# Twenty-eight experts of a PEER layer get their first product early, in plain float32

## The chip, the core and the metric

One core of a Trainium2 chip runs the whole program. The metric is the device time of one execution in microseconds (us). The engines are named as in the profile: PE (TensorE, matrix products), ACT (ScalarE), DVE (VectorE), POOL (GpSimd) and SP (SyncE, which here only issues transfers). POOL and SP both issue DMA transfers, each in a queue of its own.

## The reference, cut to what matters

Two transformer blocks on 512 tokens of width 1024. The change is in the PEER layer that ends the first block: 16384 experts, of which each token takes 8 heads x 16.

```python
def peer(h, w_query, sub_keys1, sub_keys2, expert_u, expert_v):
    q = (hf @ w_query).reshape(T, PEER_HEADS, 2, PEER_QDIM // 2)
    s1 = jnp.einsum('thc,hkc->thk', q[:, :, 0], sub_keys1)
    s2 = jnp.einsum('thc,hkc->thk', q[:, :, 1], sub_keys2)
    v1, i1 = lax.top_k(s1, PEER_TOPK)
    v2, i2 = lax.top_k(s2, PEER_TOPK)
    ...
    gate = jax.nn.softmax(vc, axis=-1)
    pre = jnp.einsum('td,tkd->tk', xb, expert_u[ib])
    a = jax.nn.gelu(pre, approximate=False) * gb
    return jnp.einsum('tk,tkd->td', a, expert_v[ib])
```

## The kernel before, in words

The 16384 experts are 128 units of 128, and the kernel calls a unit an expert `e`. For the first 384 tokens (`ND`) the layer is computed densely: for every unit a first product with `expert_u[e]` (128 experts x 384 tokens), Gelu, a multiply by a gate tile that is zero where a token did not choose the expert, and a second product with `expert_v[e]`, which is summed over all units in six PSUM banks. For the last 128 tokens the chosen rows are gathered one by one by indirect transfers, 128 of `expert_u` and 128 of `expert_v`, and DVE works each row off (`sparse`, L976).

Most products are made in three fp32r matmuls for one: both operands are split into a high part (ACT copies it, L183) and a low part (DVE subtracts, L184), and high x high, high x low and low x high are summed (`proj`, L203: 8 x 3 = 24 matmuls a unit). `wload` (L186) loads a weight unit of 512 KB on SP into one of three `wraw` buffers; `wunit` (L191) loads and splits.

The stages around the change, in program order:

- `norm_split` (L275, called at L770) computes the normalised tokens and their split `hh`, `hl`. Before it, XT is completed tile by tile (L756).
- The key search (L816 to L839): for each of 16 half heads a product with `w_query` (24 matmuls of 128x512), a piece of the modulation of the second block (`fill`, plain float32, L391), the scores against the keys (L828, plain float32) and the top 16 on DVE.
- The gates' softmax, transposes, and `pair_keys` (L878), which turns the chosen pairs into expert numbers on DVE (and POOL); `keys[0]` runs in full before the pipeline, the rest in pieces inside it.
- Gate building (L924 to L962): a pipeline of 96 items of four tokens. `g_hot` (DVE) compares, `g_wide` widens on ACT and multiplies on POOL or DVE, `g_sum` makes four plain float32 matmuls of 128x128 on PE, `g_out` copies out on ACT. Every eight items a block of 2 MB goes to DRAM (POOL's queue, L955) and a small part to the first gate tile (SP, L954).
- `u_phase` (L793) makes the first product of the first eight units (`LEAD`), with split weights.
- The loop over 128 units (L1070): in iteration e, SP loads the weights of e+10 and e+2, `prepare` (L1016) multiplies the gate into unit e+1, splits the weights of unit e+9 and the operands of unit e+1 and works off two or three gathered rows, `u_product` (L1046) makes the first product of unit e+8, `v_product` (L1054) the second of unit e (18 matmuls of 128x512).

The order of instructions on each engine is set by a list scheduler: program order is the priority, and an instruction that is ready and has its buffer may go ahead of one that is not. `tc.high_priority` lifts a part (the norm), and `pin` holds the loop's ACT and DVE instructions in program order. Each engine then runs its own list in order.

Of the kernel before, what the change touches and what calls it, by code (L numbers as in the profile page):

```python
# [107 lines left out]
def body(ctx: ExitStack, tc: tile.TileContext, a: dict, out: bass.AP, dbg=None, stop=None):  # L108
# [166 lines left out]
    def norm_split(xt, n, gcol, hh, hl, shift=None, order=None):  # L275

        with tc.high_priority():
            norm_first(xt, n, gcol, hh, hl, shift, order)

    def norm_first(xt, n, gcol, hh, hl, shift, order):  # L280
        bc = token_rstd(xt, n)
        for k in range(KT):
            h = t2(n, "nh")
            ve.scalar_tensor_tensor(h, xt[:, k], gcol[:, k:k + 1], bc, OP.mult, OP.mult)
            if shift is None:
                split_into(hh[:, k], hl[:, k], h)
            elif order is None:
                sh = shift[:, k:k + 1]
                se.activation(hh[:, k], h, AF.Identity, bias=sh)
                ve.scalar_tensor_tensor(hl[:, k], h, sh, hh[:, k].bitcast(F32), OP.add, OP.subtract)  # L290
            else:
                hs = t2(n, "nhs")
                se.activation(order[1](hs), order[0](h), AF.Identity, bias=shift[:, k:k + 1])
                split_into(hh[:, k], hl[:, k], hs)
# [469 lines left out]
    with ExitStack() as ex:  # L764
# [5 lines left out]
        norm_split(XT, T, cols[:, 8:16], hh, hl)  # L770
# [22 lines left out]
        def u_phase(e):  # L793
            ps = acc(n=ND)
            proj(ps, wunit(a["expert_u"][e]), hd_)
            t = gep.tile([128, ND], F32, name="ge")
            se.activation(t, ps, AF.Gelu)
            ge[e] = t

        with ExitStack() as gx:  # L800
# [15 lines left out]
            for hd in range(8):  # L816
                for half in range(2):
                    u = hd * 2 + half
                    keys = kp_.tile([128, 128], F32, name="keys", bufs=2)
                    gp.dma_start(keys, a["keys"][u])  # L820
                    ps = acc()
                    proj(ps, wunit(a["w_query"][u]), h)
                    fill(1 + half)
                    q = t2(name="pq")
                    se.activation(q, ps, AF.Copy)
                    st = mix([128, 4, 128], "sc")
                    for t in range(4):
                        pe.matmul(st[:, t], q[:, t * 128:(t + 1) * 128], keys, start=True, stop=True)  # L828
                    for t in range(4):
                        top16(v16[:, t, u], i16[:, t, u], st[:, t], 128, "k")  # L830
# [31 lines left out]
            hs = rows[:, RB - 1].rearrange("p (k n) -> p k n", n=128)  # L862
            ve.tensor_tensor(hs, hh[:, :, ND:].bitcast(F32), hl[:, :, ND:].bitcast(F32), OP.add)
            htok = rp.tile([128, D], F32, name="tok")
            for i in range(2):
                tps = mix([128, 4, 128], "htp")
                for k in range(4):
                    transpose(tps[:, k], hs[:, i * 4 + k])
# [3 lines left out]
        with ExitStack() as gx:  # L872
# [69 lines left out]
            def g_sum(it):  # L942
                it["ps"] = mix([128, 4, 128], "gps")
                for ti in range(4):
                    pe.matmul(it["ps"][:, ti], it["o2"][:, ti], it["o1"][:, ti], start=True, stop=True)

# [12 lines left out]
            for _ in keys[0]:  # L959
                pass  # L960
            pipeline([dict(q=th * (TG // 4) + tg, th=th, tg=tg, tok=slice(th * TG + tg * 4, th * TG + tg * 4 + 4))
                      for th in range(ND // TG) for tg in range(TG // 4)], g_hot, g_wide, g_sum, g_out)  # L962
            for e in range(LEAD):
                u_phase(e)
# [37 lines left out]
        def u_raw(e):  # L1002
            if e < NE:
# [12 lines left out]
        def prepare(eu, ev, rows_=2):  # L1016

            if ev < NE:
# [3 lines left out]
            if eu < NE:  # L1022
# [5 lines left out]
            if eu < NE:  # L1028
# [17 lines left out]
        def u_product(e):  # L1046
            if e < NE:
                ps = acc(n=ND)
                proj(ps, uw.pop(e), hd_)
                t = gep.tile([128, ND], F32, name="ge")  # L1050
                pin(se.activation(t, ps, AF.Gelu))  # L1051
                ge[e] = t
# [16 lines left out]
        prepare(NE, 0, 0)  # L1069
        for e in range(NE):  # L1070
# [4 lines left out]
            prepare(e + LEAD + 1, e + 1, 3 if e % 8 == 7 else 2)  # L1075
# [673 lines left out]
```

## Time and profile before

| what | us |
|---|---|
| median of three runs (lowest, highest) | 3473.61 (3469.06, 3474.73) |
| the profiled execution | 3477.2 |
| its span in the trace | 3475.5 |
| PE busy | 3319.4 |
| DVE busy | 2393.4 |
| ACT busy | 1265.9 |
| POOL busy | 651.4 |

The profile is of one execution, so lengths of stages and instructions are compared with its own 3477.2 us. Times in the trace count from the start of the span. A matmul's length in the trace includes its way through the array, so that matmuls in a row overlap: what one costs is read from the distance of two starts. Matmuls in fp32r appear with the type f32 in the rows.

### The profile page before, as it was taken

To read this page: it belongs to the slowest core of one execution; us is meant where nothing else is said; L and a number is where in the kernel's file an instruction comes from. 1 tells how busy PE (TensorE), PEld (TensorE's weight loads), DVE (VectorE), ACT (ScalarE), POOL (GpSimd) and SP (SyncE) were. 2 spreads that over 40 slices of the span, in tenths; PEclk is the share of its full clock that TensorE was granted. 3 is DMA by queue.
4 is the path that set the end of the run, shared out by engine and by line. 5 is a ranking of instruction groups with operands and counts; after the bars stand their busy time and mean duration, and the time that the engine had idled before them with its cause. 6 is when DMAs were issued, how large, how long until landed. Compare 5 with 4: busy or idle time off the path is not lost.

```text
span 3475.5 us, 49517 instructions
## 1 busy us (share of the span) xinstructions
PE 3319.4 (96%) x18931; PEld 2802.2 (81%) x18931; DVE 2393.4 (69%) x4746; ACT 1265.9 (36%) x2166; POOL 651.4 (19%) x676
## 2 busy tenths in 40 slices
PE   7999997679999999999999999999999999989999
PEld 4664656569999999999989887888888888878887
DVE  5544789966676776777775557587677778758776
ACT  4333213653333333333344556321211236633221
POOL 1000112653333333333311222000000002100000
PEclk9999998899999999999999999999999999999999
DMA  5345572468878888788842222121221211023331
GB/s 193 109 138 185 157 234 83 162 234 289 286 278 290 278 283 290 271 286 285 282 165 80 71 71 77 50 92 61 67 61 58 70 32 38 14 70 113 97 97 55
DMA packets 145676, 526.05 MB, mean 151 GB/s; under 512 B 17628, under 2 KB 20540, under 8 KB 143904
## 3 DMA queue, kind: packets, MB, share of 16 engines
q1 hardware_dynamic: 92880, 318.69, 28.1%
q0 software_dynamic: 52560, 204.21, 16.3%
q8 instruction: 149, 2.44, 0.3%
q14 instruction: 87, 0.71, 0.1%
HBM read 491.21 MB, written 34.10 MB: 151 GB/s over the span
## 4 chain that ended last, share of the span: by engine, by line
PE 86%; DVE 6%; DMA 3%; issue 2%; ACT 2%; POOL 1%; SPq 0%; DVEq 0%; POOLq 0%; ACTq 0%
PE pv L1061 15%; PE acc L206 12%; PE acc L208 12%; PE acc L207 12%; PE acc L232 9%; PE pd L199 3%; PE pd L201 3%; PE pd L200 3%; PE pt L347 2%; PE mod L391 2%; DMA mraw<-in_w_mod_dram 2%; DVE eb L927 1%; PE on L1351 1%; PE mix L232 1%; PE s L1312 1%
## 5 line engine op out<-in xcount | busy, mean ns | idle before, releaser
L206 PE MATMUL acc<-hh,wh 128*128 128x384 f32 (+1 forms) x1952 | 718.2, 369 | 5.2 <-DVE cg L1156 2.2
L208 PE MATMUL acc<-hh,wl 128*128 128x384 f32 (+1 forms) x1952 | 716.3, 367 | 6.0 <-DVE wl L184 6.0
L207 PE MATMUL acc<-hl,wh 128*128 128x384 f32 (+1 forms) x1952 | 715.3, 366 | 0.0
L206 PEld LDWEIGHTS acc<-hh,wh 128*128 128x128 f32 x1952 | 368.2, 189 | 64.3 <-issue 16.3
L208 PEld LDWEIGHTS acc<-hh,wl 128*128 128x128 f32 x1952 | 368.1, 189 | 53.5 <-issue 6.4
L207 PEld LDWEIGHTS acc<-hl,wh 128*128 128x128 f32 x1952 | 368.8, 189 | 46.3 <-issue 3.9
L183 ACT ACTIVATE wh<-wraw 128x1024 fp32r<-128x1024 f32 (+1 forms) x197 | 207.5, 1055 | 447.0 <-PE acc L207 249.8
L1061 PE MATMUL pv<-vh,ah 128*128 128x512 f32 x768 | 302.7, 394 | 9.5 <-DMA vraw<-in_expert_v_dram 9.5
L184 DVE TENSOR_TENSOR wl<-wraw,wh 128x1024 fp32r<-128x1024 f32 (+1 forms) x197 | 242.7, 1233 | 97.8 <-ACT wh L183 94.1
L1061 PE MATMUL pv<-vh,al 128*128 128x512 f32 x768 | 301.7, 393 | 0.0
L1061 PE MATMUL pv<-vl,ah 128*128 128x512 f32 x768 | 299.7, 390 | 0.0
L980 POOL DMA_INDIRECT rows<-in_expert_v_dram,sidx x128 | 174.3, 1362 | 312.2 <-DVE tok L995 276.8
L980 POOL DMA_INDIRECT rows<-in_expert_u_rows_dram,sidx x128 | 174.5, 1363 | 302.8 <-DVE rows L985 279.5
L1029 DVE TENSOR_TENSOR wl<-wraw,wh 128x1024 fp32r<-128x1024 f32 x120 | 149.8, 1249 | 96.5 <-ACT wh L1025 96.5
L1037 DVE TENSOR_TENSOR al<-ge,ah 128x384 fp32r<-128x384 f32 x128 | 71.4, 558 | 203.4 <-ACT ah L1035 203.4
L232 PE MATMUL acc<-wh,hh 128*128 128x256 f32 (+1 forms) x624 | 194.9, 313 | 3.9 <-ACT hh L183 2.3
L232 PE MATMUL acc<-wh,hl 128*128 128x256 f32 (+1 forms) x624 | 193.1, 309 | 0.0
L232 PE MATMUL acc<-wl,hh 128*128 128x256 f32 (+1 forms) x624 | 192.4, 308 | 0.0
L1051 ACT ACTIVATE ge<-acc 128x384 f32<-128x384 f32 x120 | 58.9, 491 | 356.6 <-PE acc L208 356.6
L1035 ACT ACTIVATE ah<-ge 128x384 fp32r<-128x384 f32 x128 | 67.0, 523 | 308.8 <-PE pv L1061 298.9
L1061 PEld LDWEIGHTS pv<-vh,ah 128*128 128x128 f32 x768 | 144.7, 189 | 35.3 <-ACT vh L1036 9.8
L1061 PEld LDWEIGHTS pv<-vh,al 128*128 128x128 f32 x768 | 144.7, 188 | 33.3
(452 smaller groups left out, 7282.3 us busy)
## 6 DMA issues: line engine op xcount, KB each, us to landing
wraw<-in_expert_u_dram SPq DMA_DIRECT2D x128, 512.0 KB, 5.4
vraw<-in_expert_v_dram SPq DMA_DIRECT2D x128, 512.0 KB, 4.0
mraw<-in_w_mod_dram SPq DMA_DIRECT2D x96, 512.0 KB, 4.3
wraw<-in_ffn_up_dram SPq DMA_DIRECT2D x88, 512.0 KB, 3.6
gt<-gdr POOLq DMA_DIRECT2D x31, 768.0 KB, 8.0
wraw<-in_ffn_down_dram SPq DMA_DIRECT2D x44, 512.0 KB, 3.7
gdr<-rows POOLq DMA_DIRECT2D x6, 2048.0 KB, 6.7
gdr<-gst POOLq DMA_DIRECT2D x6, 2048.0 KB, 7.6
```

The source lines that it names most:

```text
L183: se.activation(hi, src, AF.Copy)
L184: ve.tensor_tensor(lo, src, hi.bitcast(F32), OP.subtract)
L199: pe.matmul(ps, wh[i], xh[i], start=i == 0, stop=False)
L200: pe.matmul(ps, wh[i], xl[i], start=False, stop=False)
L201: pe.matmul(ps, wl[i], xh[i], start=False, stop=i == n - 1)
L206: pe.matmul(ps, wh[:, k], hh[:, k], start=k == 0, stop=False)
L207: pe.matmul(ps, wh[:, k], hl[:, k], start=False, stop=False)
L208: pe.matmul(ps, wl[:, k], hh[:, k], start=False, stop=k == KT - 1)
L232: pe.matmul(ps[:, i], x[:, k, s], y, start=k == 0 and i == 0 and x is hh and y is wh, stop=k == KT - 1 and i == nt - 1 and y is wl)
L980: gp.indirect_dma_start(r, None, src, bass.IndirectOffsetOnAxis(ap=sidx[:, k:k + 1], axis=0))
L1029: pin(ve.tensor_tensor(wl, raw, wh.bitcast(F32), OP.subtract))
L1061: pe.matmul(sums[t][hf], x[:, s], y[:, d], start=e == 0 and y is vh and x is ah, stop=e == NE - 1 and x is al)
```

## The change

28 units get their first product early. `early_products` is a generator of steps: for each unit it loads the raw weights and makes eight plain float32 matmuls of 128x384 with the unsplit tokens `hf`, one a step, with Gelu in the last step. `ahead(n)` takes n steps: 4 after each of the 16 query products, 10 at each of the four stops of `keys[0]`, 1 or 2 after each `g_sum`, and what is left after the pipeline. The first eight units are the LEAD units, whose `u_phase` goes; the other 20 (`SP`, units 9, 14, 20, 25, ... 113, in steps of five and six) are written to DRAM by POOL and read back by SP where the loop made their product before. For these 20 the loop neither loads nor splits `expert_u`.

The unsplit tokens are kept by writing them over XT, so XT is first stored in DRAM (`xdr1`, SP) and read back in iterations 96 to 103. The transposes for the last 128 tokens read `hf`, and the addition that rebuilt them from `hh` and `hl` goes. The gathered rows are dealt out anew: one in an iteration whose `prepare` has no weight to split, 2.38 on average in the others.

```diff
--- before.py
+++ after.py
@@ -272,15 +272,15 @@
                       start=True, stop=True)
         return bc
 
-    def norm_split(xt, n, gcol, hh, hl, shift=None, order=None):
+    def norm_split(xt, n, gcol, hh, hl, shift=None, order=None, keep=False):
 
         with tc.high_priority():
-            norm_first(xt, n, gcol, hh, hl, shift, order)
-
-    def norm_first(xt, n, gcol, hh, hl, shift, order):
+            norm_first(xt, n, gcol, hh, hl, shift, order, keep)
+
+    def norm_first(xt, n, gcol, hh, hl, shift, order, keep):
         bc = token_rstd(xt, n)
         for k in range(KT):
-            h = t2(n, "nh")
+            h = xt[:, k] if keep else t2(n, "nh")
             ve.scalar_tensor_tensor(h, xt[:, k], gcol[:, k:k + 1], bc, OP.mult, OP.mult)
             if shift is None:
                 split_into(hh[:, k], hl[:, k], h)
@@ -767,7 +767,12 @@
         pmod = pool(pp, "pmod", 1, space=PS)
         ph["mix"] = pool(pp, "pmixp", 4, space=PS)
         hh, hl = split_tile("h"), split_tile("l")
-        norm_split(XT, T, cols[:, 8:16], hh, hl)
+
+        xdr1 = dp.tile([KT, 128, T], F32, name="xdr1")
+        for k in range(KT):
+            sy.dma_start(xdr1[k], XT[:, k])
+        norm_split(XT, T, cols[:, 8:16], hh, hl, keep=True)
+        hf = XT
 
         ND, TS = T - 128, T // 128 - 1
         LEAD, RB = 8, 5
@@ -790,12 +795,33 @@
         hd_ = (hh[:, :, :ND], hl[:, :, :ND])
         ge = {}
 
-        def u_phase(e):
-            ps = acc(n=ND)
-            proj(ps, wunit(a["expert_u"][e]), hd_)
-            t = gep.tile([128, ND], F32, name="ge")
-            se.activation(t, ps, AF.Gelu)
-            ge[e] = t
+
+
+        SP = [LEAD + 1 + i * 11 // 2 for i in range(20)]
+        gedr = dp.tile([len(SP), 128, ND], F32, name="gedr")
+
+        def early_products(es):
+
+            for e in es:
+                raw = wload(a["expert_u"][e], [128, KT, 128])
+                ps = acc(n=ND)
+                for k in range(KT):
+                    pe.matmul(ps, raw[:, k], hf[:, k, :ND], start=k == 0, stop=k == KT - 1)
+                    if k < KT - 1:
+                        yield
+                t = gep.tile([128, ND], F32, name="ge") if e < LEAD else t2(ND, "gs")
+                se.activation(t, ps, AF.Gelu)
+                if e < LEAD:
+                    ge[e] = t
+                else:
+                    gp.dma_start(gedr[SP.index(e)], t)
+                yield
+
+        early = early_products(list(range(LEAD)) + SP)
+
+        def ahead(n):
+            for _ in range(n):
+                next(early, None)
 
         with ExitStack() as gx:
             mp_ = pool(gx, "mod")
@@ -821,6 +847,7 @@
                     ps = acc()
                     proj(ps, wunit(a["w_query"][u]), h)
                     fill(1 + half)
+                    ahead(4)
                     q = t2(name="pq")
                     se.activation(q, ps, AF.Copy)
                     st = mix([128, 4, 128], "sc")
@@ -859,13 +886,11 @@
                     ve.tensor_copy(gT[:, t * 128:(t + 1) * 128], tps)
                 ve.tensor_copy(ib16[:, t], i16[:, t])
 
-            hs = rows[:, RB - 1].rearrange("p (k n) -> p k n", n=128)
-            ve.tensor_tensor(hs, hh[:, :, ND:].bitcast(F32), hl[:, :, ND:].bitcast(F32), OP.add)
             htok = rp.tile([128, D], F32, name="tok")
             for i in range(2):
                 tps = mix([128, 4, 128], "htp")
                 for k in range(4):
-                    transpose(tps[:, k], hs[:, i * 4 + k])
+                    transpose(tps[:, k], hf[:, i * 4 + k, ND:])
                 se.activation(htok[:, i * 512:i * 512 + 512], tps.rearrange("p k n -> p (k n)"), AF.Copy)
             fill(25)
 
@@ -943,6 +968,7 @@
                 it["ps"] = mix([128, 4, 128], "gps")
                 for ti in range(4):
                     pe.matmul(it["ps"][:, ti], it["o2"][:, ti], it["o1"][:, ti], start=True, stop=True)
+                ahead(1 + (it["q"] % 4 == 3))
 
             def g_out(it):
                 th, tg = it["th"], it["tg"]
@@ -957,11 +983,10 @@
             gsts = {}
             keys = [pair_keys(t, gp if t else ve) for t in range(4)]
             for _ in keys[0]:
-                pass
+                ahead(10)
             pipeline([dict(q=th * (TG // 4) + tg, th=th, tg=tg, tok=slice(th * TG + tg * 4, th * TG + tg * 4 + 4))
                       for th in range(ND // TG) for tg in range(TG // 4)], g_hot, g_wide, g_sum, g_out)
-            for e in range(LEAD):
-                u_phase(e)
+            ahead(8 * len(SP))
 
         pp.close()
         b1.close()
@@ -1000,7 +1025,7 @@
         step = sparse()
 
         def u_raw(e):
-            if e < NE:
+            if e < NE and e not in SP:
                 uw[e] = wload(a["expert_u"][e], [128, KT, 128])
 
         def v_raw(e):
@@ -1015,17 +1040,18 @@
 
         def prepare(eu, ev, rows_=2):
 
+            wh = None
             if ev < NE:
                 x = ge.pop(ev)
                 pin(ve.tensor_tensor(x.rearrange("p (g t) -> p g t", t=TG), x.rearrange("p (g t) -> p g t", t=TG),
                                      gts[ev // NGR % 2][:, :, ev % NGR], OP.mult))
-            if eu < NE:
+            if eu in uw:
                 raw = uw.pop(eu)
                 wh, wl = [wp.tile([128, KT, 128], F32R, name=n, bufs=WB) for n in ("wh", "wl")]
                 pin(se.activation(wh, raw, AF.Copy))
             if rows_:
                 next(step, None)
-            if eu < NE:
+            if wh is not None:
                 pin(ve.tensor_tensor(wl, raw, wh.bitcast(F32), OP.subtract))
                 uw[eu] = wh, wl
             if ev < NE:
@@ -1045,11 +1071,13 @@
 
         def u_product(e):
             if e < NE:
-                ps = acc(n=ND)
-                proj(ps, uw.pop(e), hd_)
-                t = gep.tile([128, ND], F32, name="ge")
-                pin(se.activation(t, ps, AF.Gelu))
-                ge[e] = t
+                ge[e] = t = gep.tile([128, ND], F32, name="ge")
+                if e in SP:
+                    sy.dma_start(t, gedr[SP.index(e)])
+                else:
+                    ps = acc(n=ND)
+                    proj(ps, uw.pop(e), hd_)
+                    pin(se.activation(t, ps, AF.Gelu))
 
         def v_product(e):
             ah, al, vh, vl = vw.pop(e)
@@ -1067,12 +1095,19 @@
         v_raw(1)
         prepare(LEAD, NE, 0)
         prepare(NE, 0, 0)
+        XT = x_tiles("XT")
+        due = 0
         for e in range(NE):
             if e % NGR == 0:
                 gates(e // NGR + 1)
             u_raw(e + LEAD + 2)
             v_raw(e + 2)
-            prepare(e + LEAD + 1, e + 1, 3 if e % 8 == 7 else 2)
+            if 96 <= e < 96 + KT:
+                sy.dma_start(XT[:, e - 96], xdr1[e - 96])
+
+            due += 100 if e + LEAD + 1 in SP else 238
+            prepare(e + LEAD + 1, e + 1, due // 100)
+            due %= 100
             u_product(e + LEAD)
             v_product(e)
         for _ in step:
```

## Rows read from the trace of the kernel before

**Rows 1.** The page: busy us, share of the span and instructions by engine

```profile
PE 3319.4 (96%) x18931; PEld 2802.2 (81%) x18931; DVE 2393.4 (69%) x4746; ACT 1265.9 (36%) x2166; POOL 651.4 (19%) x676
```

**Rows 2.** Stretches: length, busy PE, PEld, DVE, ACT, POOL, then clock, DMA share, GB/s

```profile
379.00:528.00 149.00, 147.24 (x692) 91.31 (x691) 128.56 (x736) 29.73 (x39) 24.51 (x70) 1.00 0.62 204
528.00:567.20 39.20, 34.40 (x196) 31.03 (x194) 36.57 (x131) 13.50 (x18) 6.43 (x10) 1.00 0.31 97
567.20:675.00 107.80, 66.78 (x417) 61.90 (x417) 100.07 (x117) 56.40 (x100) 61.40 (x41) 0.78 0.27 111
675.00:748.60 73.60, 51.63 (x380) 46.34 (x378) 53.48 (x62) 52.35 (x94) 45.99 (x42) 0.95 0.51 201
748.60:762.60 14.00, 4.51 (x25) 4.18 (x25) 1.15 (x3) 1.64 (x3) 1.67 (x2) 0.84 0.81 309
762.60:1797.30 1034.70, 1034.66 (x5162) 938.57 (x5163) 729.14 (x899) 367.43 (x509) 376.30 (x281) 1.00 0.80 279
```

**Rows 3.** The chain of waits: start us, length, what; two iterations of the loop

```profile
782.41 4.12 PE pv L1061 x18
790.77 4.12 PE pv L1061 x18
```

**Rows 4.** Chain of waits in gate building, 568 to 748 us, shares by line

```profile
by line: DVE eb L927 21.2%; issue 19.3%; POOL o L939 14.8%; PE gps L945 9.2%; DVE o L939 8.9%; ACT o L937 4.8%; DMA gdr<-rows 4.0%; DVE eq L904 2.9%; DVE wl L1029 2.2%; DVE ic L888 2.1%; ACT rows L952 1.4%; POOL rows L980 1.3%; ACT gst L952
```

**Rows 5.** PE's groups of the whole run: the sums of gate building

```profile
L945 PE MATMUL gps<-o,o 128*128 128x128 f32 x768 | 112.4, 305 | 56.9 <-POOL o L939 29.6 <-DVE o L939 19.1 <-ACT o L937 7.3
```

**Rows 6.** PE in order of time, 91 to 98 us

```profile
91.41 1.02 PE L567 MATMUL mix<-cT,wqk_m 128*128 128x512 f32 x2
...
98.27 1.05 PE L578 MATMUL kp<-wqk_m,cT 128*128 128x128 f32 x8
```

**Rows 7.** PE in order of time, 601 to 603 us

```profile
601.39 1.95 PE L945 MATMUL gps<-o,o 128*128 128x128 f32 x16
603.10 0.42 PE L208 MATMUL acc<-hh,wl 128*128 128x384 f32 x1
```

**Rows 8.** DVE's groups in ten loop iterations, 1000 to 1083.7 us

```profile
L985 DVE SCALAR_TENSOR_TENSOR rows<-rows,tok 128x1024 f32<-128x1024 f32 x22 | 26.8, 1221 | 0.0
...
L1043 DVE TENSOR_TENSOR vl<-vraw,vh 128x1024 fp32r<-128x1024 f32 x10 | 12.2, 1221 | 0.0
...
L1037 DVE TENSOR_TENSOR al<-ge,ah 128x384 fp32r<-128x384 f32 x10 | 5.6, 558 | 16.8 <-ACT ah L1035 16.8
```

**Rows 9.** DMA issues of the whole run: KB each, us to landing

```profile
xdr<-XT SPq DMA_DIRECT2D x8, 256.0 KB, 2.3
```

**Rows 10.** DVE in order of time, 368 to 377 us

```profile
368.64 0.69 DVE L756 TENSOR_TENSOR XT<-XT,acc 128x512 f32<-128x512 f32 x1 [2.80 <-PE acc L201]
...
375.96 1.41 DVE L284 SCALAR_TENSOR_TENSOR nh<-XT,cols,nbc 128x512 f32<-128x512 f32 x2 [2.17 <-PE nbc L271]
```

**Rows 11.** DVE in order of time, 541 to 549 us

```profile
541.77 2.36 DVE L184 TENSOR_TENSOR wl<-wraw,wh 128x1024 fp32r<-128x1024 f32 x2
...
544.64 1.23 DVE L184 TENSOR_TENSOR wl<-wraw,wh 128x1024 fp32r<-128x1024 f32 x1
...
547.93 1.23 DVE L184 TENSOR_TENSOR wl<-wraw,wh 128x1024 fp32r<-128x1024 f32 x1
```

**Rows 12.** Groups in gate building, 568 to 675 us

```profile
L945 PE MATMUL gps<-o,o 128*128 128x128 f32 x391 | 61.0, 320 | 35.6 <-DVE o L939 15.1 <-POOL o L939 13.0 <-ACT o L937 7.3
...
L955 POOL DMA_DIRECT2D gdr<-rows x3 | 1.8, 598 | 0.0
```

**Rows 13.** The group of sums in gate building, 675 to 748 us

```profile
L945 PE MATMUL gps<-o,o 128*128 128x128 f32 x380 | 51.9, 290 | 21.3 <-POOL o L939 16.7 <-DVE o L939 4.0 <-ACT gst L952 0.6
```

**Rows 14.** Who waited for whom, 568 to 748.6 us: us, times, longest

```profile
PE gps L945 <- POOL o L939: 29.6, 27, 6.6
...
POOL o L939 <- PE gps L945: 26.3, 19, 3.9
```

**Rows 15.** Waits of SP's DMA queue, 375 to 765 us: us, times, longest

```profile
SPq L954 <- ACT o L937: 35.8, 1, 35.8
```


## The prediction

> **What bounds the kernel now.** I read the page first: TensorE (PE) is busy 96% of the span, the other engines far less [rows 1]. An average hides stages, so the next view is busy time by stretch [rows 2], cut at the key search (379 to 528 us), a tail in which VectorE (DVE) finishes the top 16 and the first pair keys (to 567), gate building (two stretches, to 675 and 748.6), a gap (to 762.6) and the expert loop (to 1797). The reader should see different bounds in them.
>
> The loop is bound by PE: 1034.66 of 1034.7 us. In its chain of waits a v product of 18 matmuls takes 4.12 us, and the next starts 8.36 us later [rows 3], so a u product (24 matmuls in fp32r) takes 8.36 - 4.12 = 4.24 us, 0.177 us a matmul. The key search is bound by PE as well: 147.2 of 149 us, with query products, the modulation that `fill` feeds in, and scores. In gate building PE has time left: DVE is busy 100 of 107.8 us in its first stretch [rows 2], and the chain goes round DVE, POOL, PE and ACT [rows 4].
>
> **What a plain float32 product costs.** A plain float32 matmul stands in the trace as two records: `g_sum` issues 96 x 4 = 384 matmuls, and L945 has 768 rows [rows 5]. Back to back, the 16 records of 128x512 of L567 and L570 run from 91.41 to 98.27 us, 0.429 us each [rows 6]; 16 records of 128x128 take 603.10 - 601.39 = 1.71 us, 0.107 each [rows 7]. In between, 128x384 gives 0.107 + (0.429 - 0.107) x 256/384 = 0.322 us, so a matmul costs 0.643 us and an expert's eight 5.15 us. That is an estimate from these rows, and it is 0.91 us more than the 4.24 us of the fp32r product. The early product therefore pays only where PE would stand idle, and for the splits that it spares ACT and DVE.
>
> **The change part by part**, against the profiled execution's own 3477.2 us (span 3475.5 and 1.7 around it; the median of the three runs shown is 3473.6, so 3.6 is taken off at the end).
>
> *Loop.* 20 of 120 u products go: 20 x 4.24 = -84.8 us, if the others keep up. In a thin iteration PE has 4.12 us of work. DVE's thin iteration has a gate multiply, al, vl and one row: 0.56 + 0.56 + 1.22 + 1.22 = 3.6 us; a full one, with wl and 2.38 rows, 0.56 + 0.56 + 1.22 + 1.22 + 2.38 x 1.3 = 6.7 of 8.36 [rows 8]. DVE makes wl before it waits (by ACT's ah) for PE's previous v product, the 16.8 us in front of al [rows 8], so the u product after a thin iteration finds its weights split. The rows still end near iteration 119: 20 + 100 x 2.38 = 258. Bytes: 279 GB/s x 1034.7 us = 288.7 MB, less 20 weights of 512 KB, plus 20 results of 192 KB and 2 MB of XT, is 284 MB in 950 us, 299 GB/s; the gap stretch moved 309 [rows 2]. SP issues 28 loads more and 20 fewer, with only prefetches queued behind them, two iterations ahead of their use. Bounds: -85 and, if thin iterations save half, -42; I take -84.8, since PE's rows show no wait at all there.
>
> *Key search.* `ahead(4)` after each of 16 products is 64 steps, eight experts: 8 x 5.15 = +41.2 us on a PE that has 1.8 us idle [rows 2]. They come before later projections in program order, so nothing there hides them. Bounds 35 and 45. Their eight weight loads find 38% of the DMA time free.
>
> *Norm.* XT goes to DRAM in eight stores on SP, ahead of query and modulation loads; stores like them land in 2.3 us [rows 9]. The in-place multiply of tile k waits for store k, but the last XT tile is done at 369.3 and the first multiply starts only at 375.96 [rows 10], so this costs 0; if SP stands waiting for XT and the query loads come late, up to +6.
>
> *Tail.* The LEAD splits go. Between the softmax and the pair keys DVE makes four of 1.2 us, some while it waits for the exponent [rows 11]; I count 4 of 4.8, and 1 for another that follows in gate building: -5. The five experts of `ahead(10)` need 25.7 us of PE where the LEAD products of before (30 us) go away; if the transposes for the pair keys queue behind steps, up to +6. Their Gelu runs on an ACT that is busy 13.5 of 39.2 us.
>
> *Gate building.* 120 steps (15 experts, 77 us) are written between the 96 groups of sums. Room by pitch: 107.8 - 391 x 0.107 = 66 us in the first stretch and 73.6 - 380 x 0.107 = 33 in the second [rows 2, 12, 13], so the work fits. What it costs are collisions. PE waits for POOL's operand 27 times and POOL for PE's group 19 times [rows 14]; a step of 0.643 us in front of a group delays it by 0.32 on average, and about 32 of the 96 groups lie on the chain: +10. POOL issues 20 stores of 0.6 us [rows 12], 12 us, of which I put a third on the chain: +4; a store also waits for its Gelu, with POOL's multiplies queued behind it. SP, empty there before but for twelve small stores that wait for ACT up to 36 us [rows 15], now carries the weight loads between them; three buffers cover some 10 us of such a wait, and I cost it at 0. Against this, the granted clock is 0.78 in the first stretch, so PE ran 44% of it at 1.2 GHz and not 2.4; if a third of the 42 us of sums ran there at double length (14 us) and a third of that lay on the chain, a filled PE gives back 4: -4. Term +10; bounds -8 (no collision, the clock counted twice) and +77 (every step delays the chain by its whole length).
>
> The Trainium skill (DMA: Bandwidth & Descriptors, section SWDGE vs HWDGE vs iDMA) would have plain transfers issued from SP or ACT and only irregular ones from GpSimd. By it the 20 stores belong on SP; the term of 4 us would then be 0, and the sum 4 us lower.
>
> Sum: -84.8 + 41.2 - 5 + 10 = -38.6, so 3438.6 in the profiled frame and **3435** in that of the median.
>
> **The rivals.**
>
> *Gate building stretches by the steps.* Place: PE's queue between the L945 groups; price 0.643 us for each of 120 steps, 77 us. For it: the chain there is a ring of short waits through PE [rows 4, 14]. Against it: DVE, not PE, is nearly full in the first stretch. It decides from 84.8 - 41.2 + 5 = 48.6 us on, 0.41 us a step; at full price 3473.6 - 84.8 + 41.2 - 5 + 77 = 3502, slower. The Trainium skill (TensorE: Matmul & The Clock Gate, Part 3) says that matmuls start and end in program order and that only weight loads are pulled ahead; a sum could then not overtake a step once both are queued, and no row here shows one that does.
>
> *Gate building takes the steps for nothing.* The idle time swallows them: 3473.6 - 84.8 + 41.2 - 5 - 8 = 3417. For it: 99 us of room against 77.
>
> *The loop gives half.* Row gathers, v loads or DVE hold the thin iterations: -42.4 in place of -84.8, 3477, no change. For it: DMA is 80% busy in the loop [rows 2]. Against it: DVE has 300 us to spare there.
>
> *The steps do not run where they are written*, because weights come late in the key search: then the key search grows less and gate building more. The two terms move against each other, and the time stays in the forecast's range.
>
> **How the numbers follow.** A difference of 0.2%, 7 us, is about what a measurement of this kernel can tell. The forecast has 0.62 (its own range 3418 to 3455), free steps 0.14, steps at full price 0.14, half a loop 0.10. Faster: 0.62 + 0.14 + 0.01 = 0.77; within 0.2%: 0.08, from the half loop; slower: 0.14 + 0.01 = 0.15. The range from 3412 to 3480 leaves out the dear steps and a little below.
>
> **What would show it.** In the profile after: v products 4.12 us apart in thin iterations and a loop of about 950 us; the last score (L828 before) near 569 us in place of 528; a new matmul line with 28 x 16 = 448 records at a pitch of 0.32 us; no weight split on DVE in the tail; gate building of about 190 us with the clock near 1. A pitch well off 0.32, PE idle in the loop, or a gate stage above 230 us would make the forecast wrong.

## The result, and the profile after

| | before | changed |
|---|---|---|
| median, us (lowest, highest; 4 runs each) | 3474.17 (3469.06, 3477.37) | 3432.30 (3428.61, 3436.03) |
| ratio, 95% interval | | 0.9881 [0.9864, 0.9898] |
| span of the profiled execution | 3475.5 | 3432.8 |

The changed kernel is faster by 1.2%; the forecast was 3435. The profiled execution took 3434.51 us. The page's first line, which answers to [rows 1], shows why shares alone say little: PE is 97% busy in 43 us less.

```profile
PE 3317.0 (97%) x18707; PEld 2756.1 (80%) x18707; DVE 2352.1 (69%) x4717; ACT 1242.1 (36%) x2138; POOL 679.5 (20%) x696
```

The stretches of the changed kernel, cut at the same events as [rows 2]: key search up to the last score, tail, gate building in two parts, gap, loop (length; busy PE, PEld, DVE, ACT, POOL; clock, DMA share, GB/s).

```profile
379.00:560.50 181.50, 178.64 (x812) 113.38 (x811) 127.02 (x733) 31.74 (x44) 22.39 (x70) 1.00 0.54 185
560.50:595.60 35.10, 33.34 (x116) 18.52 (x115) 32.23 (x126) 7.33 (x11) 8.67 (x15) 1.00 0.40 125
595.60:700.00 104.40, 88.26 (x479) 68.85 (x480) 88.34 (x105) 54.69 (x98) 59.85 (x46) 0.90 0.42 155
700.00:788.70 88.70, 86.16 (x527) 69.42 (x526) 55.74 (x72) 61.45 (x110) 50.85 (x50) 0.98 0.63 235
788.70:807.20 18.50, 5.39 (x27) 4.13 (x26) 2.38 (x4) 2.87 (x4) 3.24 (x4) 0.73 1.00 383
807.20:1755.30 948.10, 948.06 (x4682) 853.30 (x4683) 701.65 (x879) 339.10 (x469) 399.79 (x281) 1.00 0.83 297
```

Against before this gives a balance, in us of one profiled execution each:

| stage | before | changed | difference | forecast |
|---|---|---|---|---|
| last score of the key search at | 528.1 | 560.5 | +32.4 | +41.2 |
| tail | 39.1 | 35.1 | -4.0 | -5 |
| gate building | 181.4 | 193.1 | +11.7 | +10 |
| gap | 14.0 | 18.5 | +4.5 | none |
| loop | 1034.7 | 948.1 | -86.6 | -84.8 |
| the rest | 1678.2 | 1677.5 | -0.7 | 0 |
| span | 3475.5 | 3432.8 | -42.7 | -38.6 |

The loop is where the time came from. Its chain, in the lines that answer to [rows 3], shows a thin iteration as two v products in one piece (36 matmuls in 8.21 us) and the others 8.36 us apart:

```profile
838.48 4.12 PE pv L1089 x18
846.84 8.21 PE pv L1089 x36
859.28 4.12 PE pv L1089 x18
867.64 4.12 PE pv L1089 x18
```

The price of a plain float32 record can now be read. PE's rows in order of time near the end of gate building (start, length) show ten records of an early product from 777.62 to 780.85: 0.323 us each.

```profile
776.73 1.05 PE L970 MATMUL gps<-o,o 128*128 128x128 f32 x8
777.62 3.39 PE L809 MATMUL acc<-XT,wraw 128*128 128x384 f32 x10
780.85 2.84 PE L970 MATMUL gps<-o,o 128*128 128x128 f32 x24
```

Three terms needed an explanation: the key search, 9 us cheaper than its steps; gate building, right in size but not by its parts; and the gap, which the sum had left out.

**A tally by starts.** A record's busy time overlaps with the next one's. So for two stages the time from each PE record's start to the next one's was added up by line, with the idle time that the trace names taken off (some records are missing from a trace; their time falls to the one before).

```
key search, from 379 us   before  changed  changed, 4 buffers  before, 4 buffers
projections L206-L208       96.5     94.5                92.6               95.3
modulation L391             35.2     28.8                20.1               21.1
scores                      15.2     13.3                13.1               14.0
early products                 -     41.0                41.1                  -
transposes, idle             2.1      3.8                 1.3                6.5
sum                        149.0    181.4               168.1              136.9

gate building             before  changed  no products, stores kept  stores on SP
sums of the gates          111.2     93.1                     116.3          93.3
early products                 -     81.5                         -          77.8
LEAD products, transposes    7.3      0.5                       0.9           0.6
idle                        60.6     16.8                      58.7          16.0
sum                        179.1    191.9                     175.9         187.7
```

The columns beyond the first two are experiments that follow.

### The profile page after: what moved, and what is told of

Same layout as the page of the kernel before. It is cut to its first block, busy times and chain, and to the rows that moved or that the text cites. A ratio compares the mean times of both kernels' runs of the same rounds, so it can differ in the third digit from the quotient of the medians.

```text
span 3432.8 us, 49066 instructions
## 1 busy us (share of the span) xinstructions
PE 3317.0 (97%) x18707; PEld 2756.1 (80%) x18707; DVE 2352.1 (69%) x4717; ACT 1242.1 (36%) x2138; POOL 679.5 (20%) x696
## 3 DMA queue, kind: packets, MB, share of 16 engines
q0 software_dynamic: 53840, 208.14, 16.8%
## 4 chain that ended last, share of the span: by engine, by line
PE 88%; DVE 5%; DMA 3%; issue 2%; ACT 1%; POOL 1%; POOLq 0%; DVEq 0%; ACTq 0%; SPq 0%
PE pv L1089 15%; PE acc L206 12%; PE acc L207 12%; PE acc L208 12%; PE acc L232 9%; PE pd L199 3%; PE pd L201 3%; PE pd L200 3%; PE acc L809 3%; PE pt L347 2%; PE mod L391 2%; DMA mraw<-in_w_mod_dram 2%; PE gps L970 2%; PE on L1386 1%; PE mix L232 1%
## 5 line engine op out<-in xcount | busy, mean ns | idle before, releaser
L206 PE MATMUL acc<-hh,wh 128*128 128x512 f32 (+1 forms) x1728 | 642.6, 372 | 4.9 <-DVE cg L1191 2.2
L207 PE MATMUL acc<-hl,wh 128*128 128x512 f32 (+1 forms) x1728 | 639.7, 370 | 0.0
L208 PE MATMUL acc<-hh,wl 128*128 128x512 f32 (+1 forms) x1728 | 638.7, 370 | 0.6 <-DVE wl L1055 0.6
L206 PEld LDWEIGHTS acc<-hh,wh 128*128 128x128 f32 x1728 | 325.9, 189 | 56.3 <-issue 8.8
L207 PEld LDWEIGHTS acc<-hl,wh 128*128 128x128 f32 x1728 | 326.4, 189 | 49.5 <-issue 8.1
L208 PEld LDWEIGHTS acc<-hh,wl 128*128 128x128 f32 x1728 | 325.8, 189 | 43.4 <-issue 2.2
L184 DVE TENSOR_TENSOR wl<-wraw,wh 128x1024 fp32r<-128x1024 f32 (+1 forms) x189 | 231.8, 1227 | 100.2 <-ACT wh L183 96.6
L1005 POOL DMA_INDIRECT rows<-in_expert_v_dram,sidx x128 | 192.6, 1505 | 233.7 <-DVE tok L1020 207.7
L232 PE MATMUL acc<-wh,hl 128*128 128x256 f32 (+1 forms) x624 | 193.1, 310 | 0.0
L1069 DVE TENSOR_TENSOR vl<-vraw,vh 128x1024 fp32r<-128x1024 f32 x128 | 156.3, 1221 | 16.8 <-ACT vh L1062 16.8
L809 PE MATMUL acc<-XT,wraw 128*128 128x384 f32 x448 | 167.1, 505 | 0.0
```

Source lines behind the costliest of these rows:

```text
L184: ve.tensor_tensor(lo, src, hi.bitcast(F32), OP.subtract)
L206: pe.matmul(ps, wh[:, k], hh[:, k], start=k == 0, stop=False)
L207: pe.matmul(ps, wh[:, k], hl[:, k], start=False, stop=False)
L208: pe.matmul(ps, wl[:, k], hh[:, k], start=False, stop=k == KT - 1)
L232: pe.matmul(ps[:, i], x[:, k, s], y, start=k == 0 and i == 0 and x is hh and y is wh, stop=k == KT - 1 and i == nt - 1 and y is wl)
L809: pe.matmul(ps, raw[:, k], hf[:, k, :ND], start=k == 0, stop=k == KT - 1)
```

## The experiments

Each was compared with the kernel before on the same chip (medians there from 3471.9 to 3474.8), and each has one profile. Stages that nobody edited differ between these profiles: in the changed kernel and in experiments 2, 5, 6, 8 and 9 the last score comes between 557.4 and 564.3 us, and in the changed kernel and experiments 1, 7 and 8 gate building takes between 190.7 and 193.1 us. Smaller differences of a stage say nothing.

**1. LEAD products in the key search in fp32r.** What does the plain form cost where PE is full?

```diff
+                w = wunit(a["expert_u"][e]) if e < LEAD else None
...
+                    if w:
+                        proj(ps, w, hd_, [k])
+                    else:
                         pe.matmul(ps, raw[:, k], hf[:, k, :ND], ...)
```

> Changed kernel with the eight LEAD products of the key search made in fp32r from split weights (24 matmuls and a split each) instead of eight plain ones. Theory A, the key search pays for the PE time of what is put into it: 128 records at 0.322 us (41.2) become 192 at 0.177 (34.0), so the last score comes 7 us earlier (553.5 in place of 560.5) and the time is 3427 in place of 3434.5. Theory B, the saving of the plain products lies in the spared splits (1.06 us of ACT and 1.23 us of DVE each): the last score comes 0 to 5 us later and the time is 3434 to 3440.

Measured: 3427.34 us (3425.48 to 3432.99), ratio 0.9875 [0.9858, 0.9891]; last score at 552.8 against 560.5. In fp32r a step is three records of 0.177, so the 64 steps are worth 64 x (0.643 - 0.531) = 7.2 us less, and the last score comes 7.7 sooner, 4.6 ahead of the earliest among the kernels with an unedited key search. That speaks for A: PE pays the steps there, and the splits on ACT and DVE beside it cost nothing that shows. The intervals of the two ratios overlap; the stage carries the verdict.

**2. No steps between the gates**, and five early results in place of twenty.

```diff
-        SP = [LEAD + 1 + i * 11 // 2 for i in range(20)]
+        SP = [LEAD + 1 + i * 11 // 2 for i in range(5)]
...
-                ahead(1 + (it["q"] % 4 == 3))
```

> Changed kernel without the 120 steps in gate building: only 5 of the 20 results are made early (in the tail), the other 15 products stay in the loop. Theory A, the steps are paid for in gate building where PE is full (its second half): the loop grows by 15 x 4.24 = 63.6 us to 1012, gate building falls from 193 to about 181 us, the gap from 18 to 14, and the time is 3482. Theory B, the steps are free and gate building is longer for another reason (the 20 stores on POOL, the clock): gate building stays at 190 or more and the time is 3495. Theory C, every step lay on the chain: gate building falls by 77 us to 116 and the time is 3421.

Measured once: 3481.51 us; gate building 176.9, gap 15.3, loop 1012.8. A, with gate building shorter than it said. The 15 products between the gates and their stores cost 193.1 - 176.9 + 3.2 = 19.4 us and bring 1012.8 - 948.1 = 64.7. Without them the change would be no gain at all: what it pays in the key search is not earned back by the rest.

**3 and 4. The LEAD products after the pipeline**, in fp32r with split weights (3) or plain (4).

```diff
-                    ahead(4)
...
             ahead(8 * len(SP))
+            for e in range(LEAD):
+                u_phase(e)
```

```diff
-        early = early_products(list(range(LEAD)) + SP)
+        early = early_products(SP + list(range(LEAD)))
...
-                    ahead(4)
```

> Changed kernel with the LEAD units made as before the change (fp32r, after the pipeline in program order) and no steps in the key search; the 20 results are made early as in the changed kernel. Theory A, only the key search pays for LEAD: the last score is back at 528 us (-32), the 34 us of fp32r products go into idle PE time of the tail, gate building and the gap (33 us by the profile), and their splits cost DVE some 5 us: 3407. Theory B, PE has no room left after the key search: LEAD's 34 us come back in full and the time is 3436.

> Changed kernel with no steps in the key search and the eight LEAD units last in the order of early products, still plain float32: their 64 steps are taken after the pipeline in program order. Theory A: last score at 528 us (-32), 41.2 us of steps against 33 us of idle PE, so 8 us come back: 3410. Theory B, no room: all 41 us come back, 3443.

Measured: 3427.09 us (3424.43 to 3430.25), 0.9872 [0.9855, 0.9888], and 3430.37 (3430.31 to 3432.17), 0.9880 [0.9863, 0.9896]. Both theories missed. The key search is back where it was (last score at 526.7 and 528.1), but the gap grows to 40.5 and 51.3 us, by 22 and 33. The stretch of the gap in kernel 3 says why:

```profile
759.70:800.20 40.50, 38.34 (x216) 37.69 (x216) 9.01 (x10) 10.70 (x17) 2.21 (x3) 1.00 0.66 242
```

216 records are nine products of 24 (the loop's first was there before), 38.3 of 40.5 us: PE is full, and eight products are more than the wait of the gap can cover.

**5. The stores on SP's queue.**

```diff
-                    gp.dma_start(gedr[SP.index(e)], t)
+                    sy.dma_start(gedr[SP.index(e)], t)
```

> The 20 early results go to DRAM from SP's queue in place of POOL's; nothing else is edited. Theory A (the stores' 20 x 0.58 us on POOL stand in the way of POOL's o and gt, which bound the gate building in part): gate building (193.1 us in the changed kernel) falls by 4 to 189, time 3428 to 3430. Rival B (the second half of the gate building is bound by PE, which is busy there 86.4 of 88.9 us, so POOL's stores lie beside it): gate building within 1.5 us of 193, time 3431 to 3434.

Measured: 3431.02 us (3429.99 to 3434.05), 0.9880 [0.9864, 0.9897]; gate building 188.9, as A had it, the time as B had it. The whole time does not tell: the last score came at 563.2, 2.7 later than in the changed kernel, though nothing was edited there. In the stage the gain is 1.8 to 4.2 us against the 190.7 to 193.1 of the kernels with an unedited gate building. The waits of gate building (us, times, longest) show what the stores did. In the changed kernel POOL stood with a store for the Gelu of the same product, and its multiplies behind it:

```profile
POOL gedr L817 <- ACT gs L813: 28.6, 9, 5.3
```

With the stores on SP that wait is gone from POOL, but POOL now waits 39.1 us for the groups of sums, where it waited 15.7 before, so most of the wait only moved:

```profile
POOL o L964 <- PE gps L970: 39.1, 23, 3.9
```

The Trainium skill (DMA: Bandwidth & Descriptors, SWDGE vs HWDGE vs iDMA) would have plain transfers issued from SP or ACT. The stage agrees with it, by these 1.8 to 4.2 us.

**6. The stores without the products.**

```diff
+                if e >= LEAD:
+                    for k in range(KT - 1):
+                        yield
+                    gp.dma_start(gedr[SP.index(e)], hf[:, 0, :ND])
+                    yield
+                    continue
```

> The 20 early products that wait in DRAM are left out, and each of their stores writes 128x384 of other data, so the stores, the loads of them in the loop and the thin iterations are as in the changed kernel, and 320 records of plain float32 and 20 weight loads are gone; the outputs lack the products of these 20 experts. Theory A (what the gate building pays for, +11.7 us, is PE's time of the steps): gate building 177 as in the kernel without steps between the gates, gap 18, loop 948, time 3412 to 3418. Rival B (it is paid for the stores and POOL): gate building stays above 186, time 3425 to 3432.

Measured once: 3410.08 us; gate building 177.2, gap 15.1, loop 949.2. A in the stage, with a gap and a time below its figures: stores that wait for nothing are free, and the products are what is paid. PE's steps are not tested by themselves here, since the products' Gelus on ACT and their weight loads are gone with them. The stretches of gate building hold a second answer:

```profile
591.70:690.00 98.30, 59.49 (x360) 54.63 (x361) 91.69 (x105) 50.64 (x90) 57.91 (x37) 0.78 0.26 111
690.00:768.90 78.90, 57.76 (x413) 52.22 (x412) 60.31 (x72) 56.88 (x103) 49.50 (x44) 0.93 0.48 187
```

Without any step the granted clock is 0.78 and 0.93, near the 0.78 and 0.95 of [rows 2], and yet the stage is 4.2 us shorter than before. So those 4.2 us are not the clock's. What made them is open: of the LEAD work only one product (6.0 us of PE) and one weight split lay in the stage before.

**7. Four buffers for the modulation weights in the key search.**

```diff
-                    raw = mp_.tile([128, 2, 512], F32, name="mraw", bufs=2)
+                    raw = mp_.tile([128, 2, 512], F32, name="mraw", bufs=2 + 2 * ly)
```

> Four buffers in place of two for the raw modulation weights while the key search runs. Theory A (the early products cost 32 us there and not 41 because modulation products of four column strips fall together, a run of 8 records taking as long as a run of 4; more buffers ahead let more of them fall together): more runs of 8 than the 17 of the changed kernel, last score at 554 (560.5 before this edit), time 3425 to 3429. Rival B (the strips fall together by the order in which the steps are issued, and the buffers have no part in it): 17 runs of 8 within 2, last score 560 to 561, time 3431 to 3434.

Measured: 3421.11 us (3418.44 to 3424.07), 0.9856 [0.9839, 0.9872]; last score at 547.7. A, by more than it said. PE's rows in order of time show the mechanism. In the kernel before, the modulation runs mostly four records at a time (two matmuls, on two column strips of 32):

```profile
431.76 1.05 PE L391 MATMUL mod<-mraw,silc 128*32 128x512 f32 x4
432.74 0.50 PE L206 MATMUL acc<-hh,wh 128*128 128x512 f32 x1
```

In the changed kernel more of them come as eight (four strips):

```profile
449.89 1.07 PE L391 MATMUL mod<-mraw,silc 128*32 128x512 f32 x8
450.89 2.85 PE L809 MATMUL acc<-XT,wraw 128*128 128x384 f32 x8
```

From start to start, four records take 0.98 us and eight take 1.00. From 379 us to the last score the kernel before has 26 runs of 4 and 8 of 8, the changed one 12 and 15 (the 17 of the expectation count two from ahead of 379 us). The loads show why: the weights of the run of four at 431.76 us landed at 431.6 and those of the next pair only at 432.9, while the two loads behind the run of eight at 449.89 had both landed, at 447.2 and 449.8. With four buffers there are 9 runs of 8 and 6 of 16, none of 4, and the modulation takes 20.1 us. The Trainium skill (TensorE: Matmul & The Clock Gate, Part 3: Packing small matmuls) says that matmuls on different column tiles overlap; these rows agree, two strips costing what four do.

**8. The reload of XT late.**

```diff
-                sy.dma_start(XT[:, e - 96], xdr1[e - 96])
+                pin(se.dma_start(XT[:, e - 96], xdr1[e - 96]))
```

> The reloads of the token tiles that the late iterations read are issued from ACT's queue in iterations 96 to 103, where they are written, so they can't move up into the gap before the loop. Theory A (the gap of 18.5 us, 4.5 longer than before, is paid to these 8 transfers beside the gates' and the first v weights' transfers): gap 14 to 15, gates' read-back 8.6 us in place of 10.7, time 3428 to 3430. Rival B (the gap is longer because the gate building ends later against the v loads or the gt copies): gap 18 to 19, time 3432 to 3434.

Measured: 3431.24 us (3428.56 to 3436.25), 0.9882 [0.9865, 0.9900]; gap 17.3. Neither theory alone. The chain through the gap (start, length) in the kernel before, then in the changed one:

```profile
748.86 8.61 DMA gdr<-gst
...
758.16 4.43 DMA vraw<-in_expert_v_dram
```

```profile
788.96 10.73 DMA gdr<-gst
...
799.94 6.11 DMA vraw<-in_expert_v_dram
```

And with the reload late:

```profile
790.50 10.61 DMA gdr<-gst
...
801.37 4.99 DMA vraw<-in_expert_v_dram
```

The v weights are quicker by 1.1 us; the gates' store is not, 10.61 us for 10.73. Beside it still lie two loads of `expert_u` weights: SP's queue, in order, held them behind the last small gate transfer, which waits for the last gates. The DMA issues of the changed kernel from 785 to 812 us (KB each, median us to landing) name both companions:

```profile
gdr<-gst POOLq DMA_DIRECT2D x1, 2048.0 KB, 10.7
vraw<-in_expert_v_dram SPq DMA_DIRECT2D x4, 512.0 KB, 5.6
wraw<-in_expert_u_dram SPq DMA_DIRECT2D x2, 512.0 KB, 12.8
...
XT<-xdr SPq DMA_DIRECT2D x2, 256.0 KB, 11.7
```

**9. The steps sooner.**

```diff
-                ahead(1 + (it["q"] % 4 == 3))
+                ahead(2 if it["q"] < 48 else 1)
```

> Two steps per gate unit in the first 48 units and one after, in place of one with a second in each fourth unit: the same products, earlier in the gate building. Theory A (the first part of the gate building is set by DVE and has idle time on PE, 16.1 of 104.4 us, the second part is full on PE, 86.4 of 88.9 us; and the last weights asked for at the end compete with the gates' read-back): gate building 186 to 189 (193.1), gap 15 to 17 (18.5), time 3424 to 3429. Rival B (a step that PE takes early holds the gate sums behind it, which DVE's and POOL's next pieces wait for): gate building 193 to 198, time 3432 to 3439.

Measured: 3432.03 us (3431.08 to 3435.46), 0.9885 [0.9868, 0.9901]; gate building 194.7, gap 15.6. A for the gap, B for the gates and the time. The waits of gate building show PE waiting 17.5 us for POOL's operand in place of 9.5, and POOL's multiplies 31.4 us for the groups of sums in place of 15.7:

```profile
POOL o L964 <- PE gps L970: 31.4, 17, 3.7
PE gps L970 <- POOL o L964: 17.5, 13, 4.0
```

Steps taken early push the ring of [rows 4, 14]: up to the 385th record of the sums, half of them, the stage takes 116.1 us in place of 110.1, and from there 78.6 in place of 83.0. In the gap only one weight load is left beside the gates' store, which takes 9.98 us; the reload of XT left between 735.6 and 744.6 us, long before it.

**10. Half of the LEAD products after the pipeline**, both halves in fp32r.

```diff
+        early = early_products(list(range(LEAD // 2)) + SP)
...
-                    ahead(4)
+                    ahead(2)
...
             ahead(8 * len(SP))
+            for e in range(LEAD // 2, LEAD):
+                u_phase(e)
```

> Experts 0 to 3 take their early product in the key search from split weights (3 records of 0.177 us per step in place of 2 of 0.322), experts 4 to 7 take theirs from split weights after the gate building. Theory A (PE waits in the gap for the gates' read-back and the first v weights, so some 4 x 4.25 = 17 us of products lie beside that wait; the 8 products moved there before grew the gap by 22 us for 34 us of PE): last score at 543 (560.5 before this edit), gap 20 to 23 (18.5), loop 948, time 3415 to 3420. Rival B (the products' weights compete with the transfers that the gap waits for, so each product there is paid in full): gap 33 to 36, time 3428 to 3433.

Measured: 3420.43 us (3418.79 to 3423.99), 0.9851 [0.9835, 0.9868]; last score at 538.7, gate building 195.3, gap 25.2, where PE is busy 23.04 of 25.2 us. The gap grew by 6.7 us for 17 us of products: half of the LEAD products is about what the wait there covers. The time lies close to A, the parts do not: the key search is 4 us shorter than it said and the gap 2 longer than its range.

**11. Four buffers in the kernel before.** Is what the modulation gives back the change's merit?

> The kernel before, with four buffers in place of two for the raw modulation weights in the key search, and no early products. From start to start of PE's records there, the modulation takes 35.2 us in the kernel before, 28.8 in the changed one and 20.1 in the changed one with four buffers. Theory A (what the modulation gives back hangs on how many weights lie ready, and the early products gave it time to have them; four buffers do the same without the products): modulation 20 to 24 us, last score at 514 to 518 (528.1), time 3460 to 3464. Rival B (the early products between the runs are what lets four strips fall together; without them the key search is paced elsewhere): modulation 32 us or more, last score 524 to 529, time 3469 to 3474.

Measured: 3458.49 us (3455.29 to 3464.53), 0.9947 [0.9926, 0.9968]; last score at 516.7, modulation 21.1 us. A, with a time a little below its range. Runs of 16 records come without any early product between them:

```profile
448.72 1.92 PE L391 MATMUL mod<-mraw,silc 128*32 128x512 f32 x16
450.58 0.60 PE L828 MATMUL sc<-keys,pq 128*128 128x128 f32 x3
```

So the modulation was held by its two buffers: two strips are one buffer's worth, and the next pair waits for its weights. Early products give the loads time; more buffers do it without them. But the two do not replace each other in the stage: four buffers bring the last score forward by 11.4 us without the early products and by 12.8 with them. With four buffers on both sides the early products still move it by only 31.0 us, 516.7 to 547.7. The modulation gives back 1.0 of their 41.1 us there; idle time and transposes give 5.2, projections and scores 3.6. Whether the change is worth less with four buffers can't be told: the medians differ by 37 us (3458.5 and 3421.1), the profiled executions by 46, and the runs of the kernel before with four buffers lie 9 us apart.

**12. Four edits together**: four buffers (7), half of the LEAD products late (10), stores on SP (5), steps sooner (9).

> Four edits together: four buffers for the modulation weights, experts 0 to 3 from split weights in the key search and 4 to 7 after the gate building, the 20 stores on SP's queue, and two steps per gate unit in the first 48. Theory A (they act in different places and add up: -13 key search by the buffers, -22 by the halved products there, +7 in the gap for the 4 products, -3 for the earlier steps): last score 526 to 530, gate building 187 to 195, gap 20 to 25, time 3404 to 3411. Rival B (fewer products in the key search leave the modulation less time to have its weights, so the buffers bring little on top): last score 534 to 539, time 3413 to 3420.

Measured: 3406.69 us (3402.35 to 3408.42), 0.9799 [0.9778, 0.9820], the fastest of all, within A's time though not by A's parts: last score at 524.6, gap only 17.9, gate building 202.0. The four late products went into the last part of gate building, where PE's groups from 690 to 759.7 us have 95 of their 96 records, in three lines of which this is the first:

```profile
L206 PE MATMUL acc<-hh,wh 128*128 128x384 f32 x32 | 11.2, 351 | 0.0
...
```

## Why the prediction was right, step by step

The forecast's case came, and its sum missed by 4 us: -38.6 against -42.7. That it missed by so little is luck in part: the key search was put 8.8 us too dear and the gap of 4.5 was left out, and in gate building -4 was put down to the clock where the runs show -4.2 of another, open cause.

*Loop:* right. The thin iterations save a whole u product, -86.6 for -84.8, with PE busy 948.06 of 948.1 us; DVE and the DMA engines (0.83 of their time, 297 GB/s against the 299 worked out) kept up. The rival of half a loop is out.

*Price of a plain product:* right. 0.323 us a record, read between two other lengths as 0.322.

*Key search:* the term is mis-sized, +32.4 for +41.2. Its steps cost what was said: 41.0 us in the tally. The sentence that failed is "so nothing there hides them": nothing does, but the other matmuls did not stay as they were. The modulation gave back 6.4 us, because more of its weights lay ready in pairs and four strips ran in the time of two; scores and projections gave back 3.9 more, idle time and transposes took 1.7, and for these there is no experiment. Experiments 7 and 11 show that the modulation's time hangs on its buffers. They also show that it is not the whole account: with four buffers the modulation gives back almost nothing, and the stage still grows by only 31.0 us, since PE's idle time gives way in its place. The bounds of 35 and 45 were too narrow, since they held only PE's price and no answer by the stage. Kernels with the same key search scatter from 557.4 to 564.3 us, so the 8.8 us are good to a few.

*Norm and tail:* right. The first multiply starts at 375.15 us and not 375.96, and the tail is 4.0 us shorter.

*Gate building:* right in size, +11.7 for +10, and not by its parts. The prediction found 66 us of room in the first stretch and 33 in the second, "so the work fits", and priced collisions. But the steps are spread evenly over the groups and the room is not: 60 of the 120 steps, 38.6 us at 0.643, fell on the second half with its 33 us. There PE became what the stage waits for, busy 86.16 of 88.70 us from 700 us on. The chain of waits from 700 to 788 us, by line:

```profile
by line: PE gps L970 50.1%; PE acc L809 43.3%; POOL rows L1005 3.2%; POOL o L964 2.7%; issue 0.9%; PE ktp L347 0.1%
```

Up to the 385th of the 768 records of the sums, and from there to its end, the stage takes 107.0 and 74.3 us before, 110.1 and 83.0 in the changed kernel, 105.4 and 83.6 with the stores on SP (experiment 5) and 104.4 and 72.8 without the products (experiment 6). So the products cost 188.9 - 177.2 = 11.7, and nearly all of it, 10.8, in the second half, where the prediction had put 10 for collisions over both. The stores cost 1.8 to 4.2 (the estimate was 4); by experiment 6, where they wait for nothing and cost nothing, it is more the wait for their Gelu, which the prediction named and then did not price, than their issue. The -4 for the clock is not shown: the clock did rise, 0.78 to 0.90 in the first stretch, but a stage 4.2 us shorter is there at 0.78 too, in experiment 6, and what the clock gave back beside the steps was not separated.

*The rival of steps at full price* failed as it was priced, +11.7 for +77, and holds in part in the second half. PE does pay 81.5 us for the steps in the tally. But 43.8 us of that came out of idle time and 18.1 out of the sums of the gates, which cost 93.1 us in place of 111.2, standing more often back to back and at the faster clock (how much by each is open). Taken with the 6.8 us of LEAD products and transposes gone from there, 81.5 - 43.8 - 18.1 - 6.8 = 12.8, the growth of the stage but for its edges. The rival of free steps had the stage 8 us shorter, and it is 11.7 longer. The rival of steps that run elsewhere is out: all 128 records of the LEAD steps start before the last score.

*Gap:* a term that was left out, +4.5. The prediction counted the 28 loads of SP "with only prefetches queued behind them" and looked at where they are written. The reload of XT stands in iterations 96 to 103, but the list scheduler sent it as the tiles came free, five of the eight transfers after a wait for a step that reads the tile: six from 778.5 to 784.4 us, and one at 789.2 and one at 792.0, in the gap. The prefetches of `expert_u`, held behind the last gates, came with it, at 789.9 and 790.9. Experiment 8, without the reload there, gives back 1.2 us. In experiments 2, 6 and 9, with gaps of 15.3, 15.1 and 15.6, the reload had left long before and one weight load was left in place of two; so some 2 us more hang on the products that end late and the loads behind them, and the last 1 us is open. Kernels with an unedited gap have between 18.4 and 19.5 us (experiments 1, 5 and 7), so that these parts are rough.

## What to carry to other kernels

Price work that is moved into a full stage from its records, then ask what in that stage is waiting for data, not for the engine: here such work got cheaper when steps were put between, and cheaper still with more buffers. Count idle time where it lies and not over a stage: gate building had 60.6 us of it for 81.5 us of steps, but half of the steps went where the room was smaller than they are, 16.8 us were left unused, and the stage grew by 11.7. Follow every transfer whose tile comes free early to where a scheduler will send it, not to where it is written.

## What was not expected of the hardware

Plain float32 matmuls of 128x512 on column strips of 32 columns: four records on two strips take 0.98 us, eight on four strips 1.00, and sixteen on four strips 1.86. Of the 35.2 us that the modulation cost in the key search before, 14 went with two more buffers (experiment 11).
